# Rotary queries and keys turned by VectorE and a DRAM bounce in place of TensorE transposes, all bounces issued by SyncE

## The chip, the core and the metric

The kernel runs on one core of one Trainium2 chip. The metric is device time in microseconds (us) of one execution. A core has TensorE (PE: matmuls, with its weight loads shown as PEld), VectorE (DVE), ScalarE (ACT), GpSimd (POOL) and SyncE (SP), and 16 DMA engines that all queues share. Each engine works through its own instructions in order; SP here does nothing but issue DMAs, POOL little else.

## The reference

Two layers over 256 tokens of width 1024, all in float32. A layer is a token mixer and a SwiGLU, each followed by a residual with factor alpha and a LayerNorm:

```python
def hybrid_mixer(x, w_in, w_branch_sb, w_branch_moba, w_out):
    proj = x @ w_in
    ...
    o_sb = stick_breaking_attention(heads(q_sb, SB_HEADS), heads(k_sb, SB_HEADS), heads(v_sb, SB_HEADS))
    o_mb = moba_attention(partial_rope(heads(q_mb, MOBA_HEADS), pos),
                          partial_rope(heads(k_mb, MOBA_HEADS), pos),
                          heads(v_mb, MOBA_HEADS))
    branch_sb = merge_heads(o_sb) @ w_branch_sb
    branch_mb = merge_heads(o_mb) @ w_branch_moba
    merged = jax.nn.sigmoid(g_sb) * branch_sb + jax.nn.sigmoid(g_mb) * branch_mb
    return merged @ w_out
```

Both branches have 8 heads of 64. With 256 tokens the second branch (MoBA) is a causal softmax attention over one block; its q and k are rotated (rope) in the first 16 of each 64 columns. The SwiGLU is `(silu(x @ w_gate) * (x @ w_up)) @ w_down` with 2816 inner columns.

## The kernel before

**Three matmuls for one.** Each float32 operand is split into a rounded part `hi` and a rest `lo` (both float32r), and each product is the sum of three matmuls, hi x hi, hi x lo and lo x hi. A split is two instructions, made by `split_line`: ScalarE casts to `hi`, VectorE subtracts to get `lo`.

**The weights** come in 122 granules per layer of 128 x 1024 (512 KB), in the order of use (`WeightStream`). SP loads a granule into one of six buffers `raw` (L135), ScalarE and VectorE split it into the rings `whi` and `wlo`, which hold ten granules. SP's load into a buffer waits until VectorE has made the `lo` of the granule six places earlier. Seven granules of a layer go another way: POOL loads them into `whi` with a cast, ScalarE copies the negative to `wlo`, and POOL adds the weights into `wlo` by an accumulating DMA.

**The order of the work** is written by a planner (`Weave`). `weave.t` is the planned time of TensorE, moved on by each matmul; `act_t`, `dve_t`, `pool_t` are planned times of the other engines. The helpers `act`, `dve` and `pool` emit an instruction and return when it should be done. Side work is written as generators, such as `rope_line` or `sb_line`; each yields the planned time at which its next piece may be emitted, and `tick`, called after every three matmuls, emits what is due. So the place of an instruction in its engine's queue follows from these estimates. At run time an engine still waits, in order, for whatever its next instruction needs. `finish` emits what is left of the given generators at once.

**A layer** in order of TensorE: projections of v (stick-breaking) and q (MoBA); four pairs of stick-breaking heads, q and k (`pqk`), with the projection of k (`pk`, MoBA) after the second pair and that of v (`pu`) after the fourth; the gates (`pg`, 8 chunks c, 48 matmuls each); the branch projections (`pb`); `pw`; LayerNorm; the SwiGLU's first matrices (`pft` for four chunks token by token, then 18 chunks `pf`); `pd` (in layer 1 also `pe`); LayerNorm. The attention runs beside `pk`, `pqk`, `pu` and `pg`: two stick-breaking pairs at a time (scores `sb_s`, mask, sigmoids `keep` and `beta`, scans `inc`, then transposes `sb_pT`, split `pp`, output `sb_o`, sums `sb_f`), then the same for MoBA (`mb_s`, `mb_e`, `mb_pT`, `mb_o`, `mb_f`). `pb` is emitted after `weave.finish(sides)`, when all of the attention is.

**PSUM turns.** Pool `psC` has two banks (`bankC`). They are handed out in order by `turn`, which lets a generator go on once the bank's user of two turns before is done. The rope transposes, the outputs `sb_o` and `mb_o` (two turns each where there are two parts) and the LayerNorm's transposes use it.

**The rope step** (`rope_line`), once for each of q and k, token tile t and layer: ScalarE copies 128 tokens x 512 columns from PSUM to `tok`; VectorE rotates with four small instructions (`ra`, two of `rb`, and their sum into `tok`); after a turn, TensorE turns four blocks of 128 x 128 into PSUM (`qmb_tp`, `kmb_tp`, L436); `put` splits them into the q or k tiles, q with the scale 0.125. `weave.finish(ropes)` stands after the first gate chunk.

**The bounce** (`bounce_line`) exists in the SwiGLU's first four chunks: `h_line` makes 128 tokens x 256 columns, VectorE transposes each 32 x 32 block (`hb`), POOL stores the result to DRAM (`sg_scr`) and, after the store, issues four loads of 32 partitions each that put the blocks in their places; then the split into `h_hi`, `h_lo`. Its planned times: `MARGIN` 0.29 after the transpose, `DMA_STORE` 3.5, `DMA_LOAD` 6.0.

Of the kernel before, what the change touches and what calls it, by code (L numbers as in the profile page):

```python
# [7 lines left out]
F32 = mybir.dt.float32  # L8
F32R = mybir.dt.float32r
AF = mybir.ActivationFunctionType  # L10
OP = mybir.AluOpType
# [3 lines left out]
P = 128  # L15
# [4 lines left out]
DH = 64  # L20
WIDTH = 512
NPAIR = 4
# [12 lines left out]
class Weave:  # L35
# [11 lines left out]
    def act(self, e, n, f, *args, **kw):  # L47
        f(*args, **kw)  # L48
        self.act_t = max(self.act_t, e) + n / 1200.0 + ACT_FIXED
        return self.act_t + HOP  # L50

    def dve(self, e, n, f, *args, **kw):
        f(*args, **kw)  # L53
        self.dve_t = max(self.dve_t, e) + n / 960.0 + DVE_FIXED
        return self.dve_t + HOP

    def pool(self, e, f, *args, **kw):
        f(*args, **kw)
        self.pool_t = max(self.pool_t, e) + 0.55
        return self.pool_t + HOP  # L60
# [190 lines left out]
MARGIN = 0.29  # L251
MB_GAP = 8.85
T0 = 4.1
DMA_STORE = 3.5
DMA_LOAD = 6.0


@with_exitstack
def hybrid_trunk_kernel(ctx: ExitStack, tc: tile.TileContext, w, xT_in, x_in, ln_in,
                        ident_in, mask_in, rope_in, out):  # L260
    nc = tc.nc
# [19 lines left out]
    def unit(name, shape, dt=F32):  # L281
        return acts.tile(shape, dt, tag="u4", name=name)

    def pair_tiles(name, shape):
        return unit(name + "_hi", shape, F32R), unit(name + "_lo", shape, F32R)

    def bankM(name, shape):
        return psM.tile(shape, F32, tag="M", name=name)

    def bankC(name, shape):  # L290
        return psC.tile(shape, F32, tag="C", name=name)
# [4 lines left out]
    weave = Weave()  # L296
    taken, left = [0], {}

    def turn(e):

        was = None
        while True:
            k = taken[0] - 2
            if k >= 0 and k not in left:
                yield
            elif (e := max(e, left.get(k, 0.0))) == was:
                break
            else:
                was = e
                yield e + MARGIN  # L310
        taken[0] += 1
        return taken[0] - 1
# [3 lines left out]
    act, dve, pool = weave.act, weave.dve, weave.pool  # L316
# [19 lines left out]
        ws.dma_t += 0.36 * n  # L336
        x_there[k0] = ws.dma_t

    def split_line(hi, lo, src, n, e, scale=None):
        if scale:  # L340
            e = act(e, n, nc.scalar.activation, hi, src, AF.Copy, scale=scale)
        else:
            e = act(e, n, nc.scalar.copy, hi, src)
        yield e
        if scale:
            return dve(e, n, nc.vector.scalar_tensor_tensor, lo, src, scale, hi.bitcast(F32),
                       op0=OP.mult, op1=OP.subtract)
        return dve(e, n, nc.vector.tensor_sub, lo, src, hi.bitcast(F32))

    def x_line(k0, n):  # L350
        hi, lo = (x[:, k0:k0 + n, :].rearrange("p k (t c) -> p t k c", t=2) for x in (xT_hi, xT_lo))
        return split_line(hi, lo, raw_x(k0, n), n * S, x_there[k0])
# [5 lines left out]
    def split_piece(g, sl, e):  # L358
        hi, lo = (part[:, sl] for part in ws.parts[g])
        for _ in split_line(hi, lo, ws.raw[g][:, sl], 512, e):  # L360
            pass
# [33 lines left out]
    hi, lo = (part[:, first[0]] for part in ws.parts[0])  # L395
    e = dve(3.6, 512, nc.vector.tensor_copy, hi, ws.raw[0][:, first[0]])
# [38 lines left out]
    def transpose(o, a):  # L435
        nc.tensor.transpose(o, a, ident)  # L436
        weave.t += 0.11

    def pe_after(e):
        weave.t = max(weave.t, e)  # L440

    def pe_done():
        return weave.t + HOP
# [60 lines left out]

    ROWS = [slice(h * DH, (h + 1) * DH) for h in range(2)]

    def bounce_line(name, out, half, src, n, e, issue):

        scr = dram.tile([P, n * P], F32, tag=f"scr{n}", name=f"{name}_scr")
        e = dve(e, n * P, nc.vector.transpose, half.rearrange("p (j n b) -> p n j b", j=4, n=n),  # L510
                src.rearrange("p (n j a) -> p n j a", n=n, j=4))
        yield e + MARGIN
        e = issue(e, scr, half) + DMA_STORE
        yield e
        blocks = scr.rearrange("(i a) (j c) -> j a i c", a=32, j=4)
        for j in range(4):
            there = issue(e, out[32 * j:32 * j + 32].rearrange("a (i c) -> a i c", i=4), blocks[j])
        e = there + DMA_LOAD
        yield e
        return out.rearrange("p (i n b) -> p n i b", i=4, n=n), e  # L520

    def by_pool(e, dst, src):
        return pool(e, nc.gpsimd.dma_start, dst, src)

    def by_act(e, dst, src):
        return act(e, 400, nc.scalar.dma_start, dst, src)

    def blocked(x):
        return x.rearrange("p n (i b) -> p n i b", b=32)

    def rope_line(name, ps, t, put):

        tmp = unit(f"{name}_tok{t}", [P, 8, DH])
        e = act(pe_done(), WIDTH, nc.scalar.copy, tmp, ps.rearrange("p (h d) -> p h d", d=DH))
        yield e
        half = ROPE // 2
        a, b = (p.tile([P, n], F32, tag=tag, name=f"{name}_{tag}{t}")[:, :8 * ROPE]
                .rearrange("p (h r) -> p h r", h=8) for p, tag, n in ((page1, "ra", 240), (page2, "rb", 208)))
        cc = rope[:, t, 0, None, :].to_broadcast([P, 8, ROPE])
        s0 = rope[:, t, 1, None, :half].to_broadcast([P, 8, half])  # L540
        s1 = rope[:, t, 1, None, half:].to_broadcast([P, 8, half])
        mul = nc.vector.tensor_mul
        dve(e, P, mul, a, tmp[:, :, :ROPE], cc)
        dve(e, P // 2, mul, b[:, :, :half], tmp[:, :, half:ROPE], s0)
        dve(e, P // 2, mul, b[:, :, half:], tmp[:, :, :half], s1)
        e = dve(e, 2 * P, nc.vector.tensor_add, tmp[:, :, :ROPE], a, b)
        i = yield from turn(e)
        tp = bankC(f"{name}_tp{t}", [P, NPAIR, P])
        flat = tmp.rearrange("p h d -> p (h d)")
        pe_after(e)  # L550
        for p in range(NPAIR):
            transpose(tp[:, p, :], flat[:, p * P:(p + 1) * P])
        yield pe_done()
        left[i] = yield from put(tp, slice(t * P, (t + 1) * P), pe_done())

    def scores(pairs):

# [229 lines left out]
    for l in range(DEPTH):  # L787
        G = l * NG_LAYER
        L = f"l{l}"
# [3 lines left out]
        q_mb = pair_tiles(L + "qmb", [P, NPAIR, S])  # L793

        def put_qmb(tp, ts, e):
            return split_line(*(q[:, :, ts] for q in q_mb), tp, WIDTH, e, 0.125)

        ropes = []

# [1 line left out]
            split_v(v_sb[t], ps)  # L801

        def put_q(t, ps):
            ropes.append(weave.start(rope_line(L + "qmb", ps, t, put_qmb)))

        if l == 0:
            first_projections((f"{L}pv", f"{L}pq"), (put_v, put_q))
        else:
            for t in range(2):
                weave.finish(norms[:t + 1])  # L810
                pe_after(xT_ready[t])
                for j, put in enumerate((put_v, put_q)):
                    ps = bankM(f"{L}pvq{j}{t}", [P, WIDTH])
                    for i in range(4):
                        g = G + 4 * j + i
                        tok_major(ps, g, t, i == 0, i == 3, 2 * i)
                        if t == 1:
                            ws.allow(g + NSPLIT)
                    put(t, ps)
# [42 lines left out]
        k_mb = pair_tiles(L + "kmb", [P, NPAIR, S])  # L862

        def put_kmb(tp, ts, e):
            return split_line(*(k[:, :, ts] for k in k_mb), tp, WIDTH, e)

        both_tokens(f"{L}pk", G + 12, lambda t, ps: ropes.append(weave.start(rope_line(L + "kmb", ps, t, put_kmb))))
        sb_pair(2, G + 16)
# [31 lines left out]
        for c, b in ((0, 0), (1, 0), (0, 1), (1, 1), *((c, b) for c in range(2, KC) for b in range(2))):  # L900
            g = G + 40 + c
            hi, lo = ws.take(g)
            hi = hi.rearrange("p (b k n) -> p b k n", b=2, k=4)
            lo = lo.rearrange("p (b k n) -> p b k n", b=2, k=4)
            if b == 0:
                banks[c] = bankM(f"{L}pb{c}", [P, 2, S])
            ps, o = banks[c], (o_sb, o_mb)[b]
# [8 lines left out]
            e = dve(0.0, S, nc.vector.tensor_add, mt[:, 0, :], mt[:, 0, :], mt[:, 1, :])  # L916
# [13 lines left out]
        hb = [unit(f"{L}hb{t}", [P, 2, 2, 256]) for t in range(2)]  # L930
# [7 lines left out]
        def h_line(name, ps, j, t):  # L938
            sg = work.tile([P, 256], F32, tag="T", name=name)
            e = act(pe_done(), 256, nc.scalar.activation, sg, ps[:, :256], AF.Sigmoid)  # L940
            yield e
            dve(e, 256, nc.vector.tensor_mul, sg, sg, ps[:, :256])
            e = dve(e, 256, nc.vector.tensor_mul, sg, sg, ps[:, 256:])
            tp, e = yield from bounce_line(name, hb[t][:, j, 1, :], hb[t][:, j, 0, :], sg, 2, e, by_pool)
            ts = slice(t * P, (t + 1) * P)
            yield from split_line(*(blocked(h[:, 2 * j:2 * j + 2, ts]) for h in h_t[0]), tp, 256, e)

# [10 lines left out]
        for t in range(2):  # L958
            weave.finish(norms[:t + 1])
            pe_after(xT_ready[t])  # L960
            for j in range(2):
                ps = bankM(f"{L}pft{t}{j}", [P, 512])
# [6 lines left out]
        for c in range(NTOK_FC, NFC):  # L969
            ps = bankM(f"{L}pf{c}", [P, 2, S])  # L970
# [115 lines left out]
```

## Time and profile before

| what | value |
|---|---|
| median of 3 runs | 731.68 us (731.38 to 731.71) |
| the profiled execution's own time | 731.41 us |
| its span, first to last instruction | 729.4 us |
| PE, DVE, ACT, POOL busy | 717.7, 519.5, 392.0, 55.9 us |
| granted TensorE clock | 0.996 |
| bytes moved by the DMA engines | 145.76 MB, mean 200 GB/s |

A row of a group reads: line, engine, operation, output<-inputs, shapes, xcount | busy us, mean ns of one | idle us of the engine just before, and what ended it. A row of a tile's instructions reads: duration in ns min/median/max, start of the first and of the last in us. A row of waits reads: who waited <- for whom: us in total, times, longest us. A row of the chain reads: start us, us, what; there the time of pipelined matmuls is counted once. A row of the timeline has start us, us, engine, line, operation, and in brackets the engine's idle time before it. L48, L53 and L58 are the helpers' lines for ACT, DVE and POOL, L423 and L436 those of matmul and transpose, L563 that of the scores; so an instruction is told by its tile. A row of stretches has the stretch, its length, the busy time of PE, PEld, DVE, ACT and POOL with counts, the granted clock, the DMA engines' share, and GB/s. A row of DMA issues has the count, the KB of each and the median us from issue to landing.

### The profile page before, as it was taken

The numbers are of one execution on the slowest core, as the hardware profiler recorded it, in microseconds if no ns is written. First come the engines' busy times: TensorE is split into PE (matmuls) and PEld (weight loads), VectorE is DVE, ScalarE is ACT, GpSimd is POOL, SyncE is SP. The second block draws the span as 40 slices with busy tenths as digits, with TensorE's granted clock in tenths as the row PEclk, the third lists the DMA queues.
The fourth block names the chain that finished last, engine by engine and source line by source line (L and its number), as shares of the span: only waits on it lengthen the run. The fifth ranks groups of instructions, "written<-read, shape, count | busy, mean of one in ns | idle before, by whom it ended". The sixth has DMA issues, their size and how long they took to land.

```text
span 729.4 us, 12769 instructions
## 1 busy us (share of the span) xinstructions
PE 717.7 (98%) x5064; PEld 661.0 (91%) x5064; DVE 519.5 (71%) x784; ACT 392.0 (54%) x590; POOL 55.9 (8%) x88
## 2 busy tenths in 40 slices
PE   9999999999999999999999999999999999999994
PEld 7989899998899999988889889999888999998884
DVE  5997876698886666643678877778789766664415
ACT  5757675663564554442366656776456555554300
POOL 0001110000330000000000111100013200000001
PEclk9999999999999999999999999999999999999998
DMA  8979675356696655485258559656738765653501
GB/s 296 359 254 294 177 197 173 142 176 248 186 344 201 198 183 198 145 300 190 86 173 285 157 143 225 203 150 199 259 120 277 279 219 189 196 194 113 205 0 58
DMA packets 43419, 145.76 MB, mean 200 GB/s; under 512 B 5344, under 2 KB 7392, under 8 KB 43360
## 3 DMA queue, kind: packets, MB, share of 16 engines
q1 hardware_dynamic: 37776, 127.91, 51.3%
q0 software_dynamic: 5440, 16.78, 10.0%
q8 instruction: 40, 0.66, 0.4%
q10 hardware_dynamic: 144, 0.26, 0.1%
q14 instruction: 19, 0.16, 0.1%
HBM read 142.84 MB, written 2.10 MB: 199 GB/s over the span
## 4 chain that ended last, share of the span: by engine, by line
PE 97%; DVE 1%; issue 0%; ACT 0%; POOL 0%; POOLq 0%; DVEq 0%
PE l1pf L423 13%; PE l0pf L423 13%; PE l0pd L423 8%; PE l1pg L423 6%; PE l0pg L423 5%; PE l1pe L423 4%; PE l1pd L423 4%; PE l1pqk L423 3%; PE l0pqk L423 3%; PE l0pw L423 3%; PE l1pvq L423 3%; PE l0pft L423 3%; PE l1pw L423 3%; PE l1pft L423 3%; PE l0pb L423 3%; PE l1pb L423 3%
## 5 line engine op out<-in xcount | busy, mean ns | idle before, releaser
L53 DVE TENSOR_TENSOR wlo<-raw,whi 128x1024 fp32r<-128x1024 f32 (+1 forms) x234 | 277.9, 1203 | 79.2 <-ACT whi L48 76.1
L48 ACT CAST whi<-raw 128x1024 fp32r<-128x1024 f32 (+1 forms) x233 | 237.4, 1035 | 79.3 <-PE l0pd L423 19.5
L423 PE MATMUL l1pf<-xT_hi,wlo 128*128 128x256 f32 x288 | 79.6, 276 | 0.0
L423 PE MATMUL l1pf<-xT_hi,whi 128*128 128x256 f32 x288 | 79.6, 276 | 0.0
L423 PE MATMUL l1pf<-xT_lo,whi 128*128 128x256 f32 x288 | 79.6, 276 | 0.0
L423 PE MATMUL l0pf<-xT_hi,wlo 128*128 128x256 f32 x288 | 79.5, 276 | 0.0
L423 PE MATMUL l0pf<-xT_hi,whi 128*128 128x256 f32 x288 | 79.5, 276 | 0.0
L423 PE MATMUL l0pf<-xT_lo,whi 128*128 128x256 f32 x288 | 79.5, 276 | 0.0
L423 PEld LDWEIGHTS l1pf<-xT_hi,whi 128*128 128x128 f32 x288 | 54.1, 188 | 0.0
L423 PEld LDWEIGHTS l1pf<-xT_lo,whi 128*128 128x128 f32 x288 | 54.1, 188 | 0.0
L423 PEld LDWEIGHTS l1pf<-xT_hi,wlo 128*128 128x128 f32 x288 | 54.1, 188 | 0.0
L423 PEld LDWEIGHTS l0pf<-xT_lo,whi 128*128 128x128 f32 x288 | 54.1, 188 | 0.0
L423 PEld LDWEIGHTS l0pf<-xT_hi,whi 128*128 128x128 f32 x288 | 54.1, 188 | 0.0
L423 PEld LDWEIGHTS l0pf<-xT_hi,wlo 128*128 128x128 f32 x288 | 54.1, 188 | 0.0
L423 PE MATMUL l0pg<-xT_hi,whi 128*128 128x256 f32 x128 | 36.1, 282 | 0.0
L423 PE MATMUL l1pg<-xT_hi,whi 128*128 128x256 f32 x128 | 36.0, 281 | 0.0
L423 PE MATMUL l1pg<-xT_hi,wlo 128*128 128x256 f32 x128 | 35.5, 277 | 0.0
L423 PE MATMUL l0pg<-xT_hi,wlo 128*128 128x256 f32 x128 | 35.5, 277 | 0.0
L423 PE MATMUL l1pg<-xT_lo,whi 128*128 128x256 f32 x128 | 35.4, 277 | 0.0
L423 PE MATMUL l0pg<-xT_lo,whi 128*128 128x256 f32 x128 | 35.4, 277 | 0.0
L423 PE MATMUL l0pd<-whi,l0h_hi 128*128 128x512 f32 x88 | 34.5, 391 | 0.0
L423 PE MATMUL l0pd<-wlo,l0h_hi 128*128 128x512 f32 x88 | 34.3, 389 | 0.0
(355 smaller groups left out, 1816.9 us busy)
## 6 DMA issues: line engine op xcount, KB each, us to landing
raw<-in_w_dram SPq DMA_DIRECT2D x226, 512.0 KB, 4.4
whi<-in_w_dram POOLq DMA_DIRECT2D x14, 512.0 KB, 6.0
wlo<-in_w_dram POOLq DMA_DIRECT2D x14, 512.0 KB, 7.7
ln<-in_ln_dram SPq DMA_DIRECT2D x8, 512.0 KB, 5.8
raw<-in_w_dram SPq DMA_DIRECT2D x7, 256.0 KB, 5.5
x<-in_x_dram SPq DMA_DIRECT2D x2, 512.0 KB, 10.3
out_dram<-x SPq DMA_DIRECT2D x3, 256.0 KB, 2.2
xT_raw<-in_xT_dram SPq DMA_DIRECT2D x4, 128.0 KB, 4.1
```

The costliest lines, as they stand in the source:

```text
L48: f(*args, **kw)
L53: f(*args, **kw)
L423: nc.tensor.matmul(o, a, b, start=start, stop=stop)
```

## The change

The rope step no longer uses TensorE. `tok` becomes the first half of a tile `both` of [128, 2, 512]. The scale 0.125 of q moves into ScalarE's first copy. After the rotation the generator calls `bounce_line` with four pairs: VectorE transposes 32 x 32 blocks from the first half into the second, one DMA stores the second half to DRAM (256 KB), four DMAs load the blocks into the first half (64 KB each), and the split reads from there, through `blocked` views of the q and k tiles. No turn of `psC` is taken.

`bounce_line` loses its argument `issue`: all its DMAs, those of the SwiGLU too, are issued by SP (`nc.sync`) and no longer by POOL, and the planner counts no issue time for them. The planned times are now 2.0 from the transpose to the store (`DMA_ISSUE`), 6.0 from there to the loads, 11.0 from there to the split. The DMAs are not entered in `ws.dma_t`, the planner's time of the weight loads; they weren't before either.

```diff
-DMA_STORE = 3.5
-DMA_LOAD = 6.0
+DMA_ISSUE = 2.0
+DMA_STORE = 6.0
+DMA_LOAD = 11.0
...
-    def split_line(hi, lo, src, n, e, scale=None):
-        if scale:
-            e = act(e, n, nc.scalar.activation, hi, src, AF.Copy, scale=scale)
-        else:
-            e = act(e, n, nc.scalar.copy, hi, src)
-        yield e
-        if scale:
-            return dve(e, n, nc.vector.scalar_tensor_tensor, lo, src, scale, hi.bitcast(F32),
-                       op0=OP.mult, op1=OP.subtract)
+    def split_line(hi, lo, src, n, e):
+        e = act(e, n, nc.scalar.copy, hi, src)
+        yield e
         return dve(e, n, nc.vector.tensor_sub, lo, src, hi.bitcast(F32))
...
-    def bounce_line(name, out, half, src, n, e, issue):
+    def bounce_line(name, out, half, src, n, e):
...
-        yield e + MARGIN
-        e = issue(e, scr, half) + DMA_STORE
+        e += DMA_ISSUE
+        yield e
+        nc.sync.dma_start(scr, half)
+        e += DMA_STORE
         yield e
         blocks = scr.rearrange("(i a) (j c) -> j a i c", a=32, j=4)
         for j in range(4):
-            there = issue(e, out[32 * j:32 * j + 32].rearrange("a (i c) -> a i c", i=4), blocks[j])
-        e = there + DMA_LOAD
+            nc.sync.dma_start(out[32 * j:32 * j + 32].rearrange("a (i c) -> a i c", i=4), blocks[j])
+        e += DMA_LOAD
         yield e
...
-    def rope_line(name, ps, t, put):
-
-        tmp = unit(f"{name}_tok{t}", [P, 8, DH])
-        e = act(pe_done(), WIDTH, nc.scalar.copy, tmp, ps.rearrange("p (h d) -> p h d", d=DH))
+    def rope_line(name, ps, t, put, scale=1.0):
+
+        both = unit(f"{name}_tok{t}", [P, 2, WIDTH])
+        tmp = both[:, 0, :].rearrange("p (h d) -> p h d", d=DH)
+        e = act(pe_done(), WIDTH, nc.scalar.activation, tmp, ps.rearrange("p (h d) -> p h d", d=DH), AF.Copy,
+                scale=scale)
...
-        i = yield from turn(e)
-        tp = bankC(f"{name}_tp{t}", [P, NPAIR, P])
-        flat = tmp.rearrange("p h d -> p (h d)")
-        pe_after(e)
-        for p in range(NPAIR):
-            transpose(tp[:, p, :], flat[:, p * P:(p + 1) * P])
-        yield pe_done()
-        left[i] = yield from put(tp, slice(t * P, (t + 1) * P), pe_done())
+        tp, e = yield from bounce_line(f"{name}{t}", both[:, 0, :], both[:, 1, :], both[:, 0, :], NPAIR, e)
+        yield from put(tp, slice(t * P, (t + 1) * P), e)
...
-            return split_line(*(q[:, :, ts] for q in q_mb), tp, WIDTH, e, 0.125)
+            return split_line(*(blocked(q[:, :, ts]) for q in q_mb), tp, WIDTH, e)
...
-            tp, e = yield from bounce_line(name, hb[t][:, j, 1, :], hb[t][:, j, 0, :], sg, 2, e, by_pool)
+            tp, e = yield from bounce_line(name, hb[t][:, j, 1, :], hb[t][:, j, 0, :], sg, 2, e)
```

More of the change, by code (lines that the diff above doesn't have):

```diff
@@ L516, in bounce_line @@
         for j in range(4):
-            there = issue(e, out[32 * j:32 * j + 32].rearrange("a (i c) -> a i c", i=4), blocks[j])
-        e = there + DMA_LOAD
+            nc.sync.dma_start(out[32 * j:32 * j + 32].rearrange("a (i c) -> a i c", i=4), blocks[j])
+        e += DMA_LOAD
         yield e
         return out.rearrange("p (i n b) -> p n i b", i=4, n=n), e
[L522 to L526, printed above, removed]
     def blocked(x):
         return x.rearrange("p n (i b) -> p n i b", b=32)
-    def rope_line(name, ps, t, put):
-        tmp = unit(f"{name}_tok{t}", [P, 8, DH])
-        e = act(pe_done(), WIDTH, nc.scalar.copy, tmp, ps.rearrange("p (h d) -> p h d", d=DH))
+    def rope_line(name, ps, t, put, scale=1.0):
[3 more added lines that the diff above has]
+                scale=scale)
         yield e
@@ L803, in put_q @@
         def put_q(t, ps):
-            ropes.append(weave.start(rope_line(L + "qmb", ps, t, put_qmb)))
+            ropes.append(weave.start(rope_line(L + "qmb", ps, t, put_qmb, 0.125)))
         if l == 0:
@@ L864, in put_kmb @@
         def put_kmb(tp, ts, e):
-            return split_line(*(k[:, :, ts] for k in k_mb), tp, WIDTH, e)
+            return split_line(*(blocked(k[:, :, ts]) for k in k_mb), tp, WIDTH, e)
         both_tokens(f"{L}pk", G + 12, lambda t, ps: ropes.append(weave.start(rope_line(L + "kmb", ps, t, put_kmb))))
```

## Prediction

> **What bounds the kernel.** I read the page's shares and the chain that ended last first, then TensorE's waits, then the chain in order of time.
>
> ```profile
> span 729.4 us, 12769 instructions
> PE 717.7 (98%) x5064; PEld 661.0 (91%) x5064; DVE 519.5 (71%) x784; ACT 392.0 (54%) x590; POOL 55.9 (8%) x88
> PE 97%; DVE 1%; issue 0%; ACT 0%; POOL 0%; POOLq 0%; DVEq 0%
> ```
>
> TensorE is busy for 98% of the span and holds 97% of the chain. So what leaves TensorE's stream shortens the kernel one for one, and what is added elsewhere costs only where it makes TensorE wait. Its waits in the whole span are two:
>
> ```profile
> PE busy L380 <- DVE mhalf L375: 1.5, 1, 1.5
> PE l0mb_o L423 <- DVE pp L53: 1.0, 1, 1.0
> ```
>
> The first is the start. The second is the end of layer 0's attention. No wait on weights (whi, wlo) is among them.
>
> **Part 1: transposes off TensorE.** Layer, q or k, token tile: 2 x 2 x 2 = 8 groups of four transposes go. The chain in order of time has the eight; the first and the last, and one layer's row with single durations:
>
> ```profile
> 31.44 0.44 PE l0qmb_tp L436 x4
> 419.08 0.44 PE l1kmb_tp L436 x4
> L436 PE MATMUL l0qmb_tp<-ident,l0qmb_tok 128*128 128x128 f32 x8 | 1.2, 272 | 0.0
> ```
>
> On the chain a group takes 0.44 us, so 8 x 0.44 = 3.52 us go: 1.76 in each layer. The 272 ns of one are pipelined over the next; were the whole 272 ns of each freed, 32 x 0.272 = 8.7 us would go. The next matmul starts 0.44 us after the group began, so I take 3.52. The Trainium skill has a rule against this change: "TensorE: Matmul & The Clock Gate", Part 4, puts a transpose in a kernel's context at about 275 ns, and "VectorE: DVE Perf Modes", rules for kernel authors, advises TensorE for a full 128x128 transpose if PSUM will do as the destination. The duration of one agrees with the trace; the sum by that figure would be an estimated 8.8 us, which the chain's 0.44 us for four contradicts. For the advice no run here shows the whole price of the other path yet.
>
> **Part 2: VectorE and ScalarE.** Added are 8 transposes of 128x512. Rows of the smaller transpose and of one other operation in two widths:
>
> ```profile
> L53 DVE STREAM_TRANSPOSE l0hb<-l0sg x4: 445/445/448, 189.6 to 206.2; 128x256 f32<-128x256 f32 x4
> L53 DVE TENSOR_TENSOR l0h_lo<-l0hb,l0h_hi x4: 417/418/420, 203.8 to 220.0; 128x256 fp32r<-128x256 f32 x4
> L53 DVE TENSOR_TENSOR l0kmb_lo<-l0kmb_tp,l0kmb_hi x2: 684/688/692, 57.4 to 65.6; 128x512 fp32r<-128x512 f32 x2
> L48 ACT CAST l0kmb_hi<-l0kmb_tp x2: 582/585/588, 56.1 to 64.9; 128x512 fp32r<-128x512 f32 x2
> ```
>
> 256 columns more cost 688 - 418 = 270 ns, so one takes 0.445 + 0.27 = 0.71 us (between 0.445, if width were free, and 0.89). Eight are 5.7 us on an engine that is busy for 519.5 of 729.4: off the chain, except where attention's chain runs through VectorE. The splits stay (about 0.59 on ScalarE, 0.69 on VectorE each) but read SBUF and come later; the scale of q moves into a copy that exists already: nothing.
>
> **Part 3: DMAs.** 8 bounces of 1 store (256 KB) and 4 loads (64 KB) are new on SP's queue; 8 smaller ones of the SwiGLU part (1 + 4 each) move there from POOL. SP issues 80 more, POOL 40 fewer.
>
> ```profile
> L135 SPq DMA_DIRECT2D raw<-in_w_dram x226: 327/328/921, 7.8 to 679.7; - x113
> SPq L135 <- DVE wlo L53: 356.4, 148, 15.5
> raw<-in_w_dram SPq DMA_DIRECT2D x226, 512.0 KB, 4.4
> x<-in_x_dram SPq DMA_DIRECT2D x2, 512.0 KB, 10.3
> out_dram<-x SPq DMA_DIRECT2D x3, 256.0 KB, 2.2
> l1sg_scr<-l1hb POOLq DMA_DIRECT2D x4, 128.0 KB, 4.9
> l1hb<-l1sg_scr POOLq DMA_DIRECT2D x16, 32.0 KB, 5.1
> L423 PE MATMUL l0pf<-xT_hi,wlo 128*128 128x256 f32 x288 | 79.5, 276 | 0.0
> ```
>
> 80 issues at about 0.33 us are 26 us of a queue that waits 356 us for raw buffers: hidden by that. A store should land in 2.2 us (quiet queues, 256 KB) to 4.9 or, behind queued weights, the 10.3 us of x; a load in 5.1 to 10.3. The planner puts 6 and 11 us between, so both mostly land in time, and a wait for a late store holds the weight loads behind it on SP. What hides that is the stock of split weights: TensorE never waits for one now, and SP's longest wait for a buffer, 15.5 us, did no harm; a hold of 5 us is less. The bounces of the SwiGLU part have the 18 chunks behind them (l0pf, whose row alone, one of three kinds, has 79.5 us) before the tiles are needed: nothing.
>
> **Part 4: when q and k are there.** k of tile 1 in layer 0 is the latest. Its last rope instruction, the first scores that need it, and the places of the stick-breaking pairs on the chain:
>
> ```profile
> L53 DVE TENSOR_TENSOR l0kmb_tok<-l0kmb_ra,l0kmb_rb x2: 291/292/292, 53.4 to 55.1; 128x128 f32<-128x128 f32 x2
> 64.47 0.44 PE l0kmb_tp L436 x4
> 64.90 1.40 PE l0pqk L423 x12
> 68.36 0.70 PE l0sb_o L423 x4
> 69.07 1.57 PE l0sb_s L563 x24
> 89.54 1.57 PE l0mb_s L563 x21
> ```
>
> Its rope ends at 55.1 + 0.29 = 55.4 us; less the 0.88 of two q groups; plus 0.71 transpose, 0.21 hand-over, 2.0, 6.0 and 11.0 of the planner = 74.4; tile 0 by the same sum from 53.4 comes to 72.7. The scores of that branch begin at 89.54 - 1.76 = 87.8: 12 us to spare, so TensorE does not wait for k directly (q is earlier still; in layer 1 the gap is wider). But the two splits of k, at 56.1 and 64.9 before, now fall into the second stick-breaking pair's chain, whose scores stand at 69.07.
>
> ```profile
> 67.90 2.36 DVE L53 TENSOR_TENSOR wlo<-raw,whi 128x1024 fp32r<-128x1024 f32 x2 [0.26 <-ACT whi L48]
> 70.18 1.78 DVE L53 TENSOR_TENSOR l0sb_f<-l0sb_o,l0sb_f 64x256 f32<-64x256 f32 x4
> 71.99 1.30 DVE L53 TENSOR_TENSOR l0sb_s<-l0sb_s,mask 128x512 f32<-128x512 f32 x2
> 70.65 1.06 ACT L48 ACTIVATE wlo<-whi 128x1024 fp32r<-128x1024 f32 x1 [1.04 <-DMA whi<-in_w_dram]
> ```
>
> That adds 2 x 0.69 = 1.38 us to VectorE between mask and weights. Against it: transposes of k no longer take turns in the two psC banks, so the sums of the first pair (l0sb_o, which came at 68.36, after k's second turn at 64.47) move ahead, and their l0sb_f additions need no longer hold back the mask, which began 71.99 - 70.64 = 1.35 us after the scores' end (69.07 + 1.57). The two cancel, by these rows.
>
> **Part 5: the ends of the two attention stages.** Whether the 1.76 us of a layer arrive depends on this chain, since the branch matmuls wait for its end:
>
> ```profile
> 135.81 0.95 PE l0mb_o L423 x4
> 491.24 0.70 PE l1mb_o L423 x4
> 491.94 1.75 PE l1pg L423 x15
> ```
>
> In layer 0 TensorE has no gate matmuls left and waits 0.96 us; from 69.07 to 135.81 the chain is serial, so each us by which it grows is lost. It starts when l0pqk is done (64.90 + 1.40 = 66.3, then its split), and that moves with TensorE by 1.76. In layer 1 there are still 1.75 us of gate matmuls behind the last l1mb_o: cover for the first 1.75 us. The unknown is late landing, for ScalarE would stand in order before a k split, in front of the chain's sigmoids:
>
> ```profile
> 55.00:70.00 15.00, 15.00 (x128) 14.24 (x126) 11.48 (x17) 10.79 (x17) 2.33 (x3) 1.00 0.97 273
> 413.00:428.00 15.00, 15.00 (x114) 14.34 (x113) 10.97 (x18) 8.30 (x14) 1.45 (x2) 1.00 0.91 256
> 61.21 1.96 SPq L417 DMA_DIRECT2D x<-in_x_dram  x2
> ```
>
> The last two numbers are the DMA engines' share and GB/s: exactly where k bounces, they are 97% and 91% busy, and x is queued at 61.21, ahead of the loads of tile 1 (issued about 74.4 - 11 = 63.4). x took 10.3 us; loads behind it land at about 61.2 + 10.3 + 0.26 MB / 273 GB/s = 72.5 + 1.0, near 73.5 and just before 74.4, and a us or two later at worst. Bounds of the growth of layer 0's chain: -0.96 (the wait cannot shrink below nothing) to +3.4 (both splits, 1.38, and 2 us of landing); I take +0.5, near the cancelling rows with half a us for landing, and 0 in layer 1 (cover 1.75).
>
> **Sum.** The profiled execution took 731.41 us: 729.4 of span and 2.0 around it. -3.52 + 0.5 = -3.0 gives 728.4. The median of the runs, 731.68, is 0.27 above that execution; against runs I say 728.6. A measurement of this kernel can tell about 0.2%, 1.46 us, from no change.
>
> **Rivals.**
> A, forecast: from 731.68 - 3.52 - 0.96 = 727.2 (the wait gone as well), less the 0.3 us by which the runs of before differ, to 730.2. Chance 0.66.
> B, layer 0's chain eats its share: growth of 1.76 to 3.4 us, so that only layer 1's 1.76 and little of the rest stay: 731.68 - 3.52 + 2 to 3.4 = 730.2 to 731.6. For it: 97% DMA share, VectorE's 1.38. Against: the free psC turns. Chance 0.2, 0.05 of it above 0.2% faster.
> C, slower: the loads of k land 5 us past their due time in both layers, and ScalarE, in order, stands before the split. Layer 0 then loses 5, layer 1 5 - 1.75 = 3.25: 731.68 - 3.52 + 8.25 = 736.4. It ends slower than before once the two delays together exceed 3.52 + 1.75 = 5.3 us. For it: x's 10.3 us in the very stretch. Against: 11 us are allowed, and in layer 1 no x is loaded. Chance 0.1.
> D, the transposes free their full 272 ns: 731.68 - 8.7 = 723.0. The chain speaks against it: four in 0.44. Chance 0.02. The 275 ns of the Trainium skill's TensorE page would be this case.
> E, the DMAs add nothing but TensorE's time goes to new waits elsewhere, since every queue's order is planned anew: no change, 731.7. Only the two waits above speak for such places. Chance 0.02.
>
> Faster by over 0.2% (below 730.2): A, a quarter of B, D: 0.73. Within: the rest of B, E: 0.17. Slower: 0.1. The range 726.9 to 731.4 holds A and nearly all of B; the likeliest case's own range ends at 730.2.
>
> **What would show it.** The eight L436 groups gone and PE's instructions fewer by 32; STREAM_TRANSPOSE of 128x512 near 0.71 us, eight of them; no TensorE wait for q, k or weights; the wait at l0mb_o between 0 and 2 us; SP's waits for the stores under 6 us and ScalarE's for the loads near 0. The prediction falls if that wait exceeds 2.7 us, if layer 1 gets one above 1 us, or if a wait for wlo appears.

## The result and the profile after

| | before | after |
|---|---|---|
| median of four runs | 731.63 us (731.38 to 731.71) | 726.47 us (726.34 to 726.56) |
| the profiled execution's own time | 731.41 | 726.34 |
| its span | 729.4 | 724.5 |

The ratio is 0.993, with an interval of 0.9918 to 0.9943: 5.2 us faster. The forecast was 728.6 with a range of 726.9 to 731.4, so the gain is larger than forecast and lies 0.4 us outside the range.

The head of the page of the changed kernel, then TensorE's waits:

```profile
span 724.5 us, 12760 instructions
PE 714.0 (99%) x5032; PEld 657.0 (91%) x5032; DVE 524.1 (72%) x792; ACT 391.0 (54%) x589; POOL 33.5 (5%) x48
```

```profile
PE busy L375 <- DVE mhalf L370: 1.5, 1, 1.5
PE l0pg L418 <- DVE l0vmb L53: 0.8, 1, 0.8
```

PE has 32 instructions fewer (5064 to 5032), VectorE 8 more, POOL 40 fewer. The 1.0 us wait at l0mb_o is gone; one of 0.8 us stands elsewhere, at the gates' first matmuls.

Where the 5.07 us between the two profiled executions lie can be read from the chain in order of time of the changed kernel (start, us, what), at places that have a row in both kernels:

```profile
27.86 10.90 PE l0pqk L418 x96
134.91 21.76 PE l0pb L418 x192
361.02 6.80 PE l1pvq L418 x30
489.94 21.76 PE l1pb L418 x192
720.40 0.40 DVE x L53
```

and of the kernel before:

```profile
27.68 3.77 PE l0pqk L423 x33
...
31.88 0.36 PE l0pqk L423 x3
...
32.68 6.85 PE l0pqk L423 x60
136.76 21.83 PE l0pb L423 x192
362.94 6.80 PE l1pvq L423 x30
493.69 21.76 PE l1pb L423 x192
724.15 0.40 DVE x L53
```

| stretch | before | after | difference |
|---|---|---|---|
| start to l0pqk | 27.68 | 27.86 | +0.18 |
| l0pqk to l0pb (layer 0's attention) | 109.08 | 107.05 | -2.03 |
| l0pb to l1pvq | 226.18 | 226.11 | -0.07 |
| l1pvq to l1pb (layer 1's attention) | 130.75 | 128.92 | -1.83 |
| l1pb to VectorE's last instruction | 230.46 | 230.46 | 0 |
| that instruction's start to the end of the span | 5.25 | 4.10 | -1.15 |
| around the span (own time less span) | 2.01 | 1.84 | -0.17 |

The two attention stages give what the transposes were worth, 1.76 us each, and a little more. The last 1.15 us come from a place where no TensorE work stands: behind the last arithmetic instruction of the program. The page's chain stops there. What comes after it shows only when the closing instructions of each engine are asked for by their line (ns min/median/max, start of the first and of the last in us). Before, and then after:

```profile
L1082 POOLq DRAIN  x3: 46/102/6347, 722.3 to 729.1; - x3
L1082 SPq DRAIN  x3: 7/7/7, 727.0 to 728.9; - x3
```

```profile
L1069 POOLq DRAIN  x3: 46/93/3072, 718.5 to 724.3; - x3
L1069 SPq DRAIN  x3: 7/7/130, 723.6 to 724.0; - x3
```

Before, POOL's drain began at 722.3 and took 6.35 us, to 728.6: 1.6 us after SP had come to its own drain (727.0). After, it took 3.07 us, to 721.6: it had ended 2.0 us before SP came to its own at 723.6, and SP, which issues the stores of the output, ends last. POOL issued 68 DMAs before and 28 after.

The new instructions and DMAs of layer 0 (duration; then for DMAs KB each and median us to landing), then the waits of ScalarE and SP (us in total, times, longest us):

```profile
L53 DVE STREAM_TRANSPOSE l0qmb_tok<-l0qmb_tok x2: 711/712/714, 30.9 to 32.4; 128x512 f32<-128x512 f32 x2
L48 ACT CAST l0kmb_hi<-l0kmb_tok x2: 607/612/617, 75.0 to 78.7; 128x512 fp32r<-128x512 f32 x2
L514 SPq DMA_DIRECT2D l0kmb_tok<-l0kmb_scr x8: 325/424/476, 63.9 to 72.9; - x8
```

```profile
l0kmb_scr<-l0kmb_tok SPq DMA_DIRECT2D x2, 256.0 KB, 3.5
l0kmb_tok<-l0kmb_scr SPq DMA_DIRECT2D x8, 64.0 KB, 6.9
l1kmb_scr<-l1kmb_tok SPq DMA_DIRECT2D x2, 256.0 KB, 7.0
```

```profile
ACT l0kmb_hi L48 <- DMA l0kmb_tok<-l0kmb_scr: 2.6, 1, 2.6
SPq L514 <- DMA l1kmb_scr<-l1kmb_tok: 5.0, 1, 5.0
```

Tile 1 of k was split at 78.7 us, not at the planned 74.4: its last load was issued at 72.9, and ScalarE stood 2.6 us for it (and 1.2 us for one of q). TensorE did not.

### The profile page after: what moved, and what is told of

Its sections match the earlier page's. It is cut to its first block, busy times and chain, and to the rows that moved or that the text cites. A ratio compares the mean times of both kernels' runs of the same rounds, so it can differ in the third digit from the quotient of the medians.

```text
span 724.5 us, 12760 instructions
## 1 busy us (share of the span) xinstructions
PE 714.0 (99%) x5032; PEld 657.0 (91%) x5032; DVE 524.1 (72%) x792; ACT 391.0 (54%) x589; POOL 33.5 (5%) x48
## 3 DMA queue, kind: packets, MB, share of 16 engines
q0 software_dynamic: 4032, 14.68, 9.0%
## 4 chain that ended last, share of the span: by engine, by line
PE 96%; DVE 2%; DMA 0%; ACT 0%; issue 0%; POOL 0%; POOLq 0%; DVEq 0%
PE l1pf L418 14%; PE l0pf L418 14%; PE l0pd L418 8%; PE l0pg L418 6%; PE l1pg L418 6%; PE l1pe L418 4%; PE l1pd L418 4%; PE l1pqk L418 3%; PE l0pqk L418 3%; PE l0pw L418 3%; PE l1pvq L418 3%; PE l0pft L418 3%; PE l1pw L418 3%; PE l1pft L418 3%; PE l0pb L418 3%; PE l1pb L418 3%
```

## The experiments

Theory at the start: the gain is the transposes (about 3.5 us) plus POOL's drain, whose length follows the number of DMAs that POOL issued. Rivals: the drain has nothing to do with the time of the run and the attention stages gave all of it; or the drain follows bytes or descriptors. For the 0.8 us wait: late loads of k, or VectorE's order.

### The DMAs of the SwiGLU part alone, there and back

e1 is the changed kernel with the SwiGLU's bounces issued by POOL again (40 DMAs; the planned times stay):

```diff
-    def bounce_line(name, out, half, src, n, e):
+    def bounce_line(name, out, half, src, n, e, queue=None):
+        queue = queue or nc.sync
...
-        tp, e = yield from bounce_line(name, hb[t][:, j, 1, :], hb[t][:, j, 0, :], sg, 2, e)
+        tp, e = yield from bounce_line(name, hb[t][:, j, 1, :], hb[t][:, j, 0, :], sg, 2, e, nc.gpsimd)
```

> The changed kernel, with the SwiGLU's 8 bounces (40 DMAs) issued by POOL again; the rotary bounces stay on SP. Theory 1: POOL's final drain lasts 0.77 us plus 0.082 us for each DMA that POOL issued (from 6.35 us with 68 and 3.07 us with 28). It comes back to about 6.35 us, ends about 1.1 us after SP's last drain instead of 2.2 us before it, and the time is 726.4 + 1.1 = 727.5 us; TensorE's part of the span is unchanged. Rival: the end got shorter for another reason (SP's own last waits, the order of its queue), the drain stays near 3 us or doesn't set the end: 726.4 us.

e2 is the kernel before with only that part of the change: its SwiGLU bounces issued by SP at the new planned times, the rope's transposes still on TensorE.

```diff
-DMA_STORE = 3.5
-DMA_LOAD = 6.0
+DMA_STORE = 6.0
+DMA_LOAD = 11.0
...
-        yield e + MARGIN
+        e += 2.0
+        yield e
...
+    def by_sp(e, dst, src):
+        nc.sync.dma_start(dst, src)
+        return e
...
-            tp, e = yield from bounce_line(name, hb[t][:, j, 1, :], hb[t][:, j, 0, :], sg, 2, e, by_pool)
+            tp, e = yield from bounce_line(name, hb[t][:, j, 1, :], hb[t][:, j, 0, :], sg, 2, e, by_sp)
```

> The kernel before, with the SwiGLU's 8 bounces issued by SP at the changed kernel's planned times (2, 6, 11); q and k are still turned by TensorE. Theory 1: POOL's final drain falls from 6.35 to about 3.07 us and the time by 1.15 us, 731.6 to 730.5; TensorE's waits stay as before (1.0 at l0mb_o). Rival: the 1.15 us belong to the rotary part or to its DMAs: 731.6 us, no change.

Measured: e1 727.29 us (727.06 to 727.46), 0.8 slower than the changed kernel. e2 730.14 (729.84 to 730.63), ratio 0.9981 to the kernel before (0.9971 to 0.999), 1.4 us faster. POOL's drain in e1, and then in e2:

```profile
L1071 POOLq DRAIN  x3: 46/102/6347, 718.1 to 725.0; - x3
```

```profile
L1087 POOLq DRAIN  x3: 46/93/3072, 722.4 to 727.7; - x3
```

The drain is 6.35 us with 68 DMAs and 3.07 with 28, whichever way q and k are turned. In e1 VectorE's last group of three instructions begins at 718.85 and the span ends at 725.3; in the changed kernel 719.25 and 724.5. So e1's end is 1.2 us longer, and a last group that came 0.4 us earlier hides a part of it in the time. In e2 TensorE's waits are those of the kernel before (1.0 us at l0mb_o) and VectorE's last instruction begins at 724.29, 0.14 later than before, so its whole gain lies at the end. The DMAs that POOL no longer issues, which were costed at nothing, are worth 0.8 us (e1 against the changed kernel) to 1.4 us (e2 against the kernel before).

e3 goes the other way and gives POOL the bounces of q and k too (the same edit, with `nc.gpsimd` in the call in `rope_line` as well): 108 DMAs.

> The changed kernel with all 16 bounces issued by POOL (108 POOL DMAs instead of 28). Theory 1, drain by number of DMAs: 0.77 + 108 x 0.082 = 9.6 us, ending 4.4 us after SP's last drain: 726.4 + 4.4 = 730.8 us, more if POOL's queue delays the weights that it casts. Rival, drain by bytes or by the cast weights alone: the drain stays at 3 to 4 us and the time at 726.4 to 727.

Measured: 727.49 us (727.32 to 727.74), and a drain of 5.77 us, shorter than with 68:

```profile
L1071 POOLq DRAIN  x3: 46/102/5773, 718.5 to 725.1; - x3
```

So a straight line from 28 to 68 does not go on to 108, at least with these DMAs.

### Number or bytes

Four kernels add spare stores by POOL to the changed kernel, in the SwiGLU of layer 1, long before the end: 40 or 80, of one row (512 bytes) or of 128 rows (64 KB).

```diff
         for c in range(NTOK_FC, NFC):
             ps = bankM(f"{L}pf{c}", [P, 2, S])
+            if l == 1 and c == NTOK_FC + 2:
+                spare = dram.tile([40, P, P], F32, tag="spare", name="spare", bufs=1)
+                for i in range(40):
+                    nc.gpsimd.dma_start(spare[i, 0:1, :], ident[0:1, :])     # e5; 80 in e9
+                    nc.gpsimd.dma_start(spare[i], ident)                     # e6; 80 in e13
```

(One of the two last lines stands in each kernel; e9 and e13 have 80 in both places.)

> The changed kernel plus 40 spare POOL stores of one row (512 bytes) each to a DRAM scratch that nobody reads, issued in layer 1's pf stage, where POOL has nothing to do: 68 POOL DMAs in all, as before the change, with almost no bytes or descriptors more. Theory, drain by the number of POOL DMAs: 6.35 us, the program's end 1.1 us later, 727.5 us. Rival, drain by descriptors or bytes (all 16 bounces on POOL gave 5.77 us with 108 DMAs, which the plain number does not explain): the drain stays near 3.1 us and the time at 726.4.

> As the spare rows, but each of the 40 stores has 128 rows (64 KB): the same number of DMAs, 128 times the descriptors and bytes. By number: 6.35 us of drain and 727.5, the same as the spare rows. By descriptors: longer than the spare rows' drain, 5.5 us or more, and 727 or later; if bytes counted, 2.6 MB beside the 4.2 MB that the bounces of all kinds moved would give about 5 us.

> The changed kernel with 80 spare one-row POOL stores, 108 POOL DMAs in all, as when all 16 bounces were on POOL (which gave a drain of 5.77 us). If the drain follows the plain number: 0.77 + 108 x 0.082 = 9.6 us and about 730.9 us. If it follows the number, but folds back somewhere between 68 and 108 (entries given back on the way): again about 5.8 us and 727.0.

> The changed kernel with 80 spare POOL stores of 128 rows (64 KB) each: 108 POOL DMAs with the descriptors of real transfers. If only the number counts: 9.6 us of drain and 730.8 us, as with 80 one-row stores. If POOL gives entries back when its descriptors have filled some store, as could explain 5.77 us with all 16 bounces on POOL: under 7 us of drain and 727 to 728 us.

Measured, with the drain of each; the rows of e9 and of e13 follow the table:

| kernel | POOL's DMAs | MB on POOL's queue | drain, us | median, us |
|---|---|---|---|---|
| changed | 28 | 14.68 | 3.07 | 726.47 |
| e5, 40 of one row | 68 | 14.70 | 6.35 | 727.65 (727.36 to 728.0) |
| e6, 40 of 128 rows | 68 | 17.31 | 6.34 | 727.51 (727.12 to 727.56) |
| e9, 80 of one row | 108 | 14.73 | 9.61 | 730.78 (730.64 to 731.42) |
| e13, 80 of 128 rows | 108 | 19.93 | 5.77 | 727.41 (726.94 to 727.47) |

```profile
L1073 POOLq DRAIN  x3: 46/102/9612, 718.6 to 728.7; - x3
```

```profile
L1073 POOLq DRAIN  x3: 46/102/5767, 719.1 to 725.4; - x3
```

Up to 68 DMAs it is the number alone: 0.02 MB more and 2.63 MB more give the same 6.35 us. From 28 to 68 to 108 DMAs with one-row stores a DMA costs 0.082 us (3.27 us for each 40); carried on to no DMA at all, that leaves an estimated 0.78. With 128 rows each the drain at 108 falls back to 5.77, as in e3 with its large bounces. The number of packets does not tell the two apart: POOL's queue has 6592 of them in e9 and in e13. So at 108 the number alone no longer gives the length; why large stores shorten it, these runs do not show. The time follows the drain once it ends after SP: e9 is 4.3 us slower than the changed kernel by stores that were all issued by 586 us of a span of 729 and that nothing reads.

### The wait that is left, and what the bounce costs

e4 moves the planned load of x from 60 to 100 us, out of the stretch where k bounces.

```diff
     def late_loads():
...
-        yield 60.0
+        yield 100.0
```

> The changed kernel, with the load of x (2 x 512 KB) planned at 100 us instead of 60, so that it no longer stands in SP's queue just ahead of the loads of k's tile 1 in layer 0. Theory: those loads land about 3 us earlier, ScalarE's wait of 2.6 us for them and TensorE's wait of 0.8 us at the gates go, and the time falls by 0.8 to 725.6 us. Rival: TensorE's 0.8 us come from VectorE's added work in the stick-breaking chain (two splits, 1.4 us), whatever lands when: 726.4 us.

Measured: 726.4 us (726.09 to 726.72). The loads of k came earlier, and yet TensorE's wait is as it was. ScalarE's and TensorE's waits in e4:

```profile
ACT l0kmb_hi L48 <- DMA l0kmb_tok<-l0kmb_scr: 0.3, 1, 0.3
PE l0pg L418 <- DVE l0vmb L53: 0.8, 1, 0.8
```

So late landing is not its cause. The timeline of VectorE (start, us) points to another: in the changed kernel a split of k stands in VectorE's order directly ahead of the split of v (l0vmb) that frees the bank for the gates. The row after these two is of e16, a kernel of the section after this one, in which that split of k stands behind l0vmb.

```profile
78.27 0.68 DVE L53 TENSOR_TENSOR l0kmb_lo<-l0kmb_tok,l0kmb_hi 128x512 fp32r<-128x512 f32 x1
78.87 0.68 DVE L53 TENSOR_TENSOR l0vmb<-l0pu,l0vmb 128x512 fp32r<-128x512 f32 x1
```

```profile
78.31 0.69 DVE L53 TENSOR_TENSOR l0vmb<-l0pu,l0vmb 128x512 fp32r<-128x512 f32 x1
```

There l0vmb begins 0.56 us earlier, and the wait is 0.2 us instead of 0.8: the place of that split is worth 0.6 us. It is not the only thing that can make this wait. In e7 both splits of k stand behind l0vmb too, but the whole stick-breaking chain runs later, l0vmb begins at 79.16, and TensorE waits 1.1 us.

e10 leaves the whole turn out: no VectorE transpose, no DRAM; the splits read the rotated tile as it stands, so q and k are not transposed.

```diff
-        tp, e = yield from bounce_line(f"{name}{t}", both[:, 0, :], both[:, 1, :], both[:, 0, :], NPAIR, e)
+        tp = both[:, 0, :].rearrange("p (i n b) -> p n i b", i=4, n=NPAIR)
+        yield e + MARGIN
```

> The changed kernel without any turning of q and k: no VectorE transpose and no bounce, the split reads the rotated tile as it stands, so the scores are computed from tiles that aren't transposed and that part of the computation is left out. It shows what the bounce path still costs. Theory: nothing but TensorE's 0.8 us wait in layer 0, behind the late k splits: 725.6 us. Rival: the bounces cost more (weights late, chains longer) and the time falls to 724 or less; or they cost nothing at all and it stays at 726.4.

Measured: 726.08 us (725.54 to 726.09), 0.4 less than the changed kernel and between the theory and the rival. Its chain:

```profile
87.82 1.57 PE l0mb_s L551 x21
134.10 0.94 PE l0mb_o L418 x4
135.04 21.82 PE l0pb L418 x192
489.96 21.82 PE l1pb L418 x192
720.47 0.40 DVE x L53
```

The last three rows stand within 0.13 us of the changed kernel's 134.91, 489.94 and 720.40. The span ends at 724.2 instead of 724.5, and SP comes to its closing drain at 723.4 instead of 723.6: the 0.4 us lie behind the last arithmetic, not in the attention. So in the order that each kernel has, the turn by VectorE and DRAM costs TensorE's path nothing that can be measured here. But the orders differ. e10 has its first l0mb_s at 87.82, as the prediction's Part 4 wanted it, then needs 46.3 us to the last l0mb_o, and TensorE waits 1.0 us there. The changed kernel has them at 90.54 and 131.44, 40.9 us apart, and its wait of 0.8 us is at the gates. What the turn would cost in an unchanged order, e10 does not show.

### The planned times

Five kernels change only the planned time from the loads to the split, for all bounces: 16, 13, 12, 10 and 9 us instead of 11. One has 9 with x at 100. One has the times of the kernel before for all three, with everything on SP.

```diff
-DMA_LOAD = 11.0
+DMA_LOAD = 16.0     # e7; 13.0 in e12, 12.0 in e16, 10.0 in e15, 9.0 in e14 and e11
```

```diff
-DMA_ISSUE = 2.0
-DMA_STORE = 6.0
-DMA_LOAD = 11.0
+DMA_ISSUE = 0.29    # e8
+DMA_STORE = 3.5
+DMA_LOAD = 6.0
```

> The changed kernel with 16 us planned from the loads to the split instead of 11. Theory: TensorE's wait of 0.8 us at the gates is VectorE's backlog in layer 0's second stick-breaking chain (the two k splits of 0.68 us stand before the split of v, l0vmb). The splits now come 5 us later, behind that chain: the wait falls to under 0.3 us, and the time to 725.7 us. Rival: the backlog is that of the chain itself and the wait stays at 0.8: 726.4.

> The changed kernel with the planned times of before (0.29 to the store, 3.5 to the loads, 6.0 to the split), all bounces on SP. Theory: the stores take 2.5 to 7 us and the loads 4.4 to 8.4, so SP stands before late stores with weight loads behind it, and ScalarE before late loads in the middle of the attention: TensorE's waits grow by some us, 728 to 733 us. Rival: the stock of split weights and the cover behind both attention stages take that too, and the time stays within 0.5 us of 726.4.

> The changed kernel with 9 us planned from the loads to the split and x loaded at 100 us: k's splits in layer 0 come 2 us earlier, with the loads no longer behind x. Theory that only VectorE's order around the second stick-breaking pair matters: the splits move ahead of the scans, the mask comes later by up to 1.4 us, TensorE's wait stays between 0.5 and 2 us: 726 to 728 us. Rival, that late landing was the cause: the wait goes, 725.6.

> The changed kernel with 13 us from the loads to the split, between 11 (726.4 us) and 16 (730.6 us). Theory: any place in that chain costs about the same, and the 730.6 us came from one wait of over 2 us at the end of layer 0's attention; at 13 that wait is between 0 and 1 us: 725.7 to 727.5 us. Rival: later is steadily worse: 728 us.

> The changed kernel with 9 us from the loads to the split and x at 60 us as it was. If the place of the splits made 742 us of the run with x at 100: 738 to 745 us here too, with TensorE waits of several us at the gates and at the ends of both attention stages. If the later x did it: 726 to 728 us.

> The changed kernel with 10 us from the loads to the split. If 11 is a lone good value because each value gives another order on VectorE: anything from 726 to 740 us, with one or more TensorE waits above 2 us in layer 0. If 11 is the edge of a good range downward: 726 to 727 us.

> The changed kernel with 12 us from the loads to the split, between 11 (726.4) and 13 (about 730). If each value gives another order: 726 to 732 us, whatever its neighbours do. If the cost grows steadily with lateness: 728 us. A wait of 2 us or more at l0mb_o would come with a lowered granted clock just behind it, about 1.5 us beyond the wait itself.

| planned load | median, us | TensorE's waits at l0pg, l0mb_o, l1mb_o (profiled execution) |
|---|---|---|
| 6 (e8, all three times old) | 747.13 (745.48 to 748.12) | 1.1, 4.1, none; 3.2 and 1.2 at l1sb_s, 2.8 at l0pu, 0.8 at l0sb_pT |
| 9 (e14) | 742.96 (741.32 to 744.6) | 5.8, 3.2, 2.6 |
| 9, x at 100 (e11) | 742.27 (741.07 to 743.48) | 4.9, 3.2, 2.6 |
| 10 (e15) | 726.33 (726.2 to 726.47) | 1.0, none, none |
| 11 (changed) | 726.47 (726.34 to 726.56) | 0.8, none, none |
| 12 (e16) | 732.52 (730.64 to 733.16) | 0.2, 2.6, 1.0 |
| 13 (e12) | 731.11 (729.28 to 731.41) | 0.2, 2.6, 1.0 |
| 16 (e7) | 730.57 (729.72 to 731.9) | 1.1, 2.6, none |

I had expected small steps; there are cliffs on both sides. In e7, e11 and e12 the theory and its rival both missed, and e8 was slower than its theory's 728 to 733. e14 and e15 came as one of their two cases said; e16 lies half a us above its 726 to 732. Below 10 the splits stand in ScalarE's order ahead of data that is not there. In e14 ScalarE waits 5.2 us for loads of q in layer 0, and TensorE then 5.8 us at the gates; that the one is passed on to the other is argued, not followed step by step. For e14's 2.6 us at l1mb_o there is no such late load: ScalarE waits for no q or k in layer 1. e8, with the old times, is slower than the kernel before by a ratio of 1.0215 (1.0197 to 1.0233). ScalarE's and SP's waits in e8:

```profile
ACT l1kmb_hi L48 <- DMA l1kmb_tok<-l1kmb_scr: 10.2, 2, 7.3
SPq L514 <- DMA l1kmb_scr<-l1kmb_tok: 14.2, 2, 7.3
```

Its span is 20.2 us longer than the changed kernel's. TensorE's waits, without the one at the start, are 13.2 - 0.8 = 12.4 us more, and its busy time is 722.3 - 714.0 = 8.3 us more, at a mean granted clock of 0.985 instead of 0.997; the two together make 20.7, about the difference. So estimates longer than the old ones are a part of the change that it cannot do without. e11 against e14 shows again that x is not the matter.

Above 11 no data is late: in e16, e12 and e7 ScalarE waits for no load of q or k. There the planner writes another order in the MoBA half of layer 0's attention. The second scores of that half and VectorE's masking of them, in the changed kernel (from the chain and from the timeline of VectorE) and then in e16 (from the chain; start, us):

```profile
111.18 1.57 PE l0mb_s L550 x24
112.11 1.38 DVE L53 TENSOR_TENSOR l0mb_s<-l0mb_s,mask 128x512 f32<-128x512 f32 x2 [1.04 <-PE l0mb_s L550]
```

```profile
113.36 1.48 PE l0mb_s L550 x22
117.57 1.22 DVE wlo L53
118.78 1.21 DVE l0mb_s L53 x2
```

In the changed kernel the mask begins 0.9 us after the scores. In e16 two weight splits stand ahead of it in VectorE's order (the second is the chain's row), VectorE idles 2.96 us for the input of the first, and the mask begins 5.4 us after the scores. From the first l0mb_s to the last l0mb_o the half takes 40.9 us in the changed kernel and in e15, 46.3 in the kernel before and in e10, and 47.2 in e16, e12 and e7; there TensorE waits 2.6 us at l0mb_o. In e7 the same wait is followed by a low clock (stretch, its length, busy us of PE, PEld, DVE, ACT, POOL, granted clock, DMA share, GB/s), and l0pb, right behind it, takes 23.40 us on the chain instead of 21.76:

```profile
132.00:138.00 6.00, 3.44 (x26) 3.10 (x25) 5.08 (x8) 3.27 (x7) 0.00 (x0) 1.00 0.78 252
138.00:142.00 4.00, 4.00 (x23) 4.00 (x22) 2.11 (x5) 2.51 (x7) 0.00 (x0) 0.57 0.78 277
```

In the profiled executions of e12 and e16 the clock stays at 1.00 in this stretch after the same wait, although a low one had been expected of e16. e12's took 729.57 us, and five of its seven others took 731.1 to 731.4; the mean granted clock is 0.993 to 0.994 in four of these five and 0.996 in all the rest. e16's took 731.0; the six executions at 732.2 to 733.2 have 0.995 to 0.996, the two at 730.6 and 731.0 have 0.997. That fits a low clock in most executions, but no trace shows where in them it lay. No planned time beats the changed kernel: 10 us is equal to it.

## Why the prediction was right and where it was wrong

**Part 1, right, a little small.** The transposes were said to give 3.52 us, 0.44 for a group. The groups are gone, and TensorE's path gained that, plus 0.25 us that remain when the wait of 0.80 instead of 0.96 us is taken off as well. A part of this is that a group also broke the stream of matmuls: the 96 matmuls l0pqk of layer 0 took 3.77 + 0.36 + 6.85 = 10.98 us around two groups and take 10.90 in one piece. Rival D (8.7 us) is out; four transposes in 0.44 us was the right price.

**Part 2, right.** 0.71 us was worked out for the VectorE transpose of 128x512; 0.711 to 0.714 was measured. Eight of them, 5.7 us of VectorE, cost TensorE's path nothing that e10 could measure. On the advice quoted from the Trainium skill, "VectorE: DVE Perf Modes", rules for kernel authors (TensorE for a full 128x128 transpose), the price of the other path is now there: in this kernel, where TensorE is the bound, the way through VectorE and DRAM took 0.4 us more than no turn at all (e10), and VectorE's last instruction came 724.15 - 720.40 = 3.8 us earlier than with TensorE's transposes. Both hold for the orders that the planner wrote, of which Part 5 says more.

**Part 3, the step that failed: "POOL 40 fewer", costed at nothing.** The end of the program has a wait of its own that stood in no list of waits and on no chain: POOL's drain, which was 0.082 us longer for each DMA from 28 to 68. It set the end before and does not after: 1.15 us of the 5.07. It is the larger of the two misses that carried the result out of the range: with POOL's 40 DMAs put back (e1) the changed kernel takes 727.29 us, which lies inside 726.9 to 731.4. The warning stood in the rows: VectorE's last instruction began at 724.15 in a span of 729.4, and 5.25 us lay behind it that the prediction never asked about. SP's side held: its waits for stores reached 5.0 us, the 5 that had been called harmless, and no weights came late. "ScalarE's waits for the loads near 0" was wrong (2.6 us for k, 1.2 for q), without a wait of TensorE for them.

**Part 4, the mechanism right, the cancelling not.** TensorE waits for no q or k. The sums of the first pair did move ahead: l0sb_o came at 68.36 us before, and now

```profile
62.26 0.70 PE l0sb_o L418 x4
...
90.54 1.57 PE l0mb_s L550 x21
```

But the MoBA scores l0mb_s, at 89.54 before, came at 90.54, though TensorE had lost 1.76 us of work on the way and had started 0.18 later: this half of the chain grew by 1.0 + 1.76 - 0.18 = 2.6 us, near Rival B's figure. Only 0.8 us of that was a wait; the planner put gate matmuls into the rest. Two steps before it were off too. The loads of k's tile 1 were to be issued at 63.4 us and were issued from 70.44 on, after SP had stood 3.6 us before them. And the landing sum as it stands, 61.2 + 10.3 and 0.26 MB at 273 GB/s, comes to 72.5, not 73.5: its last us is counted twice. ScalarE could begin the split only at 78.7.

**Part 5, the second step that failed: "each us by which it grows is lost", taken as +0.5.** The chain is not a fixed sum behind a fixed start. The MoBA half, from the first l0mb_s to the last l0mb_o, took 135.81 - 89.54 = 46.3 us before and 131.44 - 90.54 = 40.9 after, for the planner wrote another order of the same work. The chain's last rows in layer 0:

```profile
131.44 0.70 PE l0mb_o L418 x4
132.14 2.77 PE l0pg L418 x24
134.91 21.76 PE l0pb L418 x192
```

Where TensorE had waited with nothing left, it has 24 gate matmuls behind the last l0mb_o now. So the term was 0.80 - 0.96 = -0.16 instead of +0.5. That this was the order's doing, and no virtue of the bounce, is what the runs with 12, 13 and 16 us show: same DMAs, another order, 2.6 us of wait. e10, without any bounce, has a wait of 1.0 at l0mb_o as before. It was also luck: nobody had asked the planner for a shorter half. With the 46.3 us of before, the last l0mb_o would have come at an estimated 90.54 + 46.3 = 136.8 us instead of 131.44, and l0pb would have begun about 2.8 us later, a growth inside Rival B's 1.76 to 3.4 us. Layer 1 went as said: 1.83 us gained, no wait.

**The sum.** -3.0 was forecast on the profiled execution, -5.07 came: 0.66 more from layer 0's chain, 0.25 left over on TensorE's path (the broken stream a part of it), 1.15 from POOL's drain, 0.17 around the span, less 0.18 for a later start. Rivals B and C did not come: landing was late (the split at 78.7 for 74.4), but less than C's 5 us in the measured place, and e8 and e14, whose planned times are not C's, show what data that is not there when its split is due can cost: 742 to 747 us. That is above C's price of 736.4, which had neither a lower clock behind a wait nor further waits in it.

## What to carry to other kernels

Ask for the last microseconds by name: what stands between the last arithmetic instruction and the end of the span, on every queue, and count the DMAs of the engine that drains longest; 40 issues moved off it were worth as much here as TensorE's longest wait inside. Where TensorE was the bound, the transposes in its stream cost their time on the chain one for one, and the longer way through another engine and DRAM cost next to nothing, because its data was due later than it landed and because the order around it came out well. An order that a planner writes from estimates answers to them in cliffs, so a change of an estimate has no price per us: only a run tells it.

## What the hardware showed that was not expected

POOL's closing drain grew with the number of DMAs that POOL had issued in the whole program: 3.07, 6.35 and 9.61 us for 28, 68 and 108, with one-row stores as much as with 64 KB ones up to 68. With 108 large ones it was 5.77 twice (e3, e13); why is open.

After a pause of TensorE of 2.6 us at l0mb_o the granted clock was 0.57 for some 4 us in one execution (e7) and 1.00 in two other kernels' (e12, e16). After 2.6 us at l1mb_o the next 4 us had 0.71 in e14 and 0.70 in e11; after 3.2 to 3.3 us at l0mb_o they had 0.50 in e14 and e11 and 0.61 in e8, and l0pb took 23.3 to 23.9 us instead of 21.76. After the pauses of 0.8 us (the changed kernel) and 1.0 us (the kernel before, e10) the next 4 us had 1.00.
